# A streamed weight's low half made by an adding transfer instead of a subtraction, and two output-projection tiles interleaved

## The chip, the cores and the metric

The kernel runs on one core of a Trainium2 chip. The metric is the device time of one execution in microseconds; before the change it is 893.74 us, the median of 3 runs (893.54 to 894.2).

## The reference

One layer of a streaming encoder on 512 positions with 1024 channels. Two branches share a normalised input and one input projection: an RWKV-7 recurrence and a chunked gated delta rule. Their outputs are projected, gated, summed and sent through an output projection; then follow a gated MLP with a causal convolution and a last norm. Cut to what matters here, the matrix products:

```
u = rms_norm(x, norm1_g);  p = u @ w_in                       # 1024 x 5888 and a few columns
y_a = rwkv7_mix(p_rwkv, ...) @ rwkv_proj                       # 512 x 1024
y_b = gated_deltanet_mix(qkv, z, ...) @ gdn_proj               # 512 x 1024
mixed = sigmoid(gate_a) * y_a + sigmoid(gate_b) * y_b
x = x + mixed @ w_out                                          # 1024 x 1024
h = causal_depthwise_conv(rms_norm(x, norm2_g) @ ffn_up, w)    # 1024 x 5632
x = x + (silu(h_gate) * h_up) @ ffn_down                       # 2816 x 1024
return rms_norm(x, final_g)
```

All of it is float32. Each large product is computed in three passes of a shorter float format (float32r): a number a is split into a high half, a rounded to that format, and a low half, a minus the high half. The kernel adds low x high, high x high and high x low.

## The kernel before

Everything is kept transposed: channels on the 128 partitions, the 512 positions along the free dimension. A large product goes tile by tile: 128 output channels at a time, whose weights for all inputs are one tile of 128 x 1024 floats (512 KB), called a unit.

`unit` (lines 162 to 170) streams one unit. SP loads it into `raw`, a ring of two buffers. Then for each 512 columns `halves_of` (lines 152 to 160) makes the two halves: ScalarE copies to `hi` (line 156), and the subtraction raw - hi gives `lo` (line 158), every second one on GpSimd and the others on VectorE. `hi` and `lo` are rings of four buffers (HB = 4), that is two units' worth. `mm3` (line 173 on) then runs 12 matmuls for each such half: for each of the four input blocks low x high (line 180) and high x high (line 181), then four times high x low (line 183). So the first matmul of a half needs its `lo`.

The order of the program is: the first tiles (`first_tiles`), a hand-written order of recurrence steps, gates and projections in `mixing` (the table ORDER), the two branch projections (`project`), the output projection (`merge`, lines 967 on), 44 tiles of up-projection (`causal_conv3`), and the down projection (`down_pair`), which takes four pairs of output tiles; a part of it is a fast matrix product with `pair_weights`, the rest (`plain`) streams units whose last half has only 256 columns. The very last output tile is computed in two halves of 256 positions, so that its result can be normalised and stored in two pieces. A scheduler sets each engine's order; most of `unit` runs at high priority, ahead of its place in the program, as far as the rings allow. Each engine works through its own queue in order, and an instruction that waits holds up those behind it.

In `merge` the eight output tiles come one after the other, each with both of its halves. Their input `uh`, `ul` is the sum of the gated branches, made channel block by channel block by the second branch projection: the first half of a tile needs blocks 0 to 3, the second 4 to 7.

Of the kernel before, what the change touches and what calls it, by code (L numbers as in the profile page):

```python
# [9 lines left out]
F32 = mybir.dt.float32  # L10
F32R = mybir.dt.float32r
BF16 = mybir.dt.bfloat16
AF = mybir.ActivationFunctionType
ALU = mybir.AluOpType
# [3 lines left out]
D = 1024  # L18
# [76 lines left out]
class Body:  # L95
# [53 lines left out]
        self.second = False  # L149


    def halves_of(self, raw, o, w=512):
        nc = self.nc
        hi = self.stream.tile([128, 512], F32R, tag="hi", name=self.nm("hi"), bufs=HB)
        lo = self.stream.tile([128, 512], F32R, tag="lo", name=self.nm("lo"), bufs=HB)
        nc.scalar.activation(hi[:, 0:w], raw[:, o:o + w], AF.Copy)  # L156
        self.halves += 1
        self.on(str(self.halves % 4)).tensor_tensor(out=lo[:, 0:w], in0=raw[:, o:o + w], in1=hi[:, 0:w].bitcast(F32),  # L158
                                                    op=ALU.subtract)
        return hi, lo, w // 128  # L160

    def unit(self, src, n=1024, ahead=True):
        nc = self.nc
        parts = []
        with self.tc.high_priority() if ahead else nullcontext():
            raw = self.stream.tile([128, 1024], F32, tag="raw", name=self.nm("raw"), bufs=2)
            nc.sync.dma_start(out=raw[:, 0:n], in_=src)
            for o in range(0, n, 512):
                parts.append(self.halves_of(raw, o, min(512, n - o)))
        return parts  # L170


# [779 lines left out]
    def merge(self):  # L952
        nc, tc = self.nc, self.tc
        x1 = self.x1 = self.x1p.tile([128, KD, T], F32, name="x1")
        self.acc2 = self.x1p.tile([128, T], F32, name="acc2")
        for k in range(KD):
            nc.sync.dma_start(out=x1[:, k, :], in_=self.a["xT"][k])
        mh, ml = self.uh, self.ul
        with tc.tile_pool(name="proj", bufs=1, reuse_waits="tile") as pp:
            yh = pp.tile([128, 4, T], F32R, name="yh")  # L960
            yl = pp.tile([128, 4, T], F32R, name="yl")
            for i in range(4):
                self.split(yh[:, i, :], yl[:, i, :], self.yf[:, 4 + i, :], scale=0.5)
            self.project(1, lambda k: (yh[:, k, :], yl[:, k, :]))
        self.u2p = self.pool("u2p", bufs=1, reuse_waits="tile")
        self.u2h = self.u2p.tile([128, KD, T], F32R, name="u2h")
        self.u2l = self.u2p.tile([128, KD, T], F32R, name="u2l")
        for m in range(KD):
            parts = self.unit(self.a["w_out"][m])
            ps = self.bank("D")  # L970
            self.mm3(ps, parts, lambda k: (mh[:, k, :], ml[:, k, :]))
            x = x1[:, m, :]
            g = self.vec("norm2", m)
            with tc.high_priority():
                nc.vector.tensor_tensor(out=x, in0=ps, in1=x, op=ALU.add)
                nc.scalar.activation(self.u2h[:, m, :], x, AF.Copy, scale=g)
                nc.vector.scalar_tensor_tensor(out=self.u2l[:, m, :], in0=x, scalar=g, in1=self.u2h[:, m, :].bitcast(F32),
                                               op0=ALU.mult, op1=ALU.subtract)
            self.sumsq(self.acc2, x, m == 0)
# [267 lines left out]
```

## Time and profile before

| what | value |
|---|---|
| median of 3 runs | 893.74 us |
| the profiled execution | 897.17 us |
| its span, first to last instruction | 895.0 us |
| TensorE busy | 860.9 us, 96% |
| VectorE busy | 646.0 us, 72% |
| ScalarE busy | 473.2 us, 53% |
| GpSimd busy | 209.7 us, 23% |
| transfers, mean over the span | 94 GB/s |

The profile comes from one execution. Busy times say how much of the span an engine had an instruction running; matmuls overlap, so a busy TensorE may still have room. Where an engine's idle time is named with another engine, that one's instruction came last. PE is TensorE, DVE is VectorE, ACT is ScalarE, POOL is GpSimd, SP issues the transfers.

### The profile page before, as it was taken

How to read it: one execution, taken by the hardware profiler on the slowest of the kernel's cores; microseconds unless marked ns; L12 is line 12 of the kernel's file. 1: busy time of each engine (PE TensorE's matmuls, PEld its weight loads, DVE VectorE, ACT ScalarE, POOL GpSimd, SP SyncE). 2: the span in 40 equal slices, each digit the busy share in tenths (PEclk: the TensorE clock that was granted, in tenths of full speed). 3: DMA queues.
4: the chain of work that ended last, by engine and by line, in shares of the span. 5: the costliest groups of instructions: out<-in, count | busy, mean ns of one | idle time of the engine just before them, and what ended most of it. 6: DMA issues, size and time to landing. Idle time of an engine off the chain costs nothing.

```text
span 895.0 us, 13509 instructions
## 1 busy us (share of the span) xinstructions
PE 860.9 (96%) x5046; PEld 677.9 (76%) x5046; DVE 646.0 (72%) x1247; ACT 473.2 (53%) x909; POOL 209.7 (23%) x189
## 2 busy tenths in 40 slices
PE   7989999999999999999999999999999999999996
PEld 4867677666767777667787878888888888898895
DVE  6898797874888986855476448988866666573565
ACT  7745457667443777673543455455444444444433
POOL 2231123111121221111212222222222222352431
PEclk9999999999999999999999999999999999999998
DMA  7321222121212221125352323323333332332333
GB/s 263 112 91 59 71 71 72 48 73 48 72 59 71 71 72 37 60 89 206 94 174 85 94 95 94 95 94 95 94 100 101 101 100 90 99 102 86 110 86 133
DMA packets 29746, 84.25 MB, mean 94 GB/s; under 512 B 3312, under 2 KB 5488, under 8 KB 29680
## 3 DMA queue, kind: packets, MB, share of 16 engines
q1 hardware_dynamic: 29680, 83.39, 29.3%
q8 instruction: 40, 0.66, 0.3%
q14 instruction: 26, 0.21, 0.1%
HBM read 77.61 MB, written 5.77 MB: 93 GB/s over the span
## 4 chain that ended last, share of the span: by engine, by line
PE 70%; DVE 19%; ACT 4%; issue 4%; DMA 1%; POOL 1%; SPq 0%; DVEq 0%; POOLq 0%; ACTq 0%
PE D L183 15%; PE D L180 15%; PE D L181 15%; PE D L1077 5%; PE A L1077 4%; PE B L1077 3%; DVE lo L158 2%; DVE R L534 1%; DVE P L769 1%; DMA raw<-w_in 1%; DVE invN L563 1%; DVE BK L513 1%; DVE invY L565 1%; DVE BK L508 1%; DVE R L948 1%
## 5 line engine op out<-in xcount | busy, mean ns | idle before, releaser
L158 POOL TENSOR_TENSOR lo<-raw,hi 128x512 fp32r<-128x512 f32 x124 | 170.3, 1373 | 614.4 <-ACT hi L156 590.6
L156 ACT ACTIVATE hi<-raw 128x512 fp32r<-128x512 f32 x248 | 152.9, 620 | 195.7 <-PE D L183 95.2
L180 PE MATMUL D<-uh,lo 128*128 128x512 f32 x384 | 158.3, 413 | 3.5 <-ACT uh L204 1.9
L181 PE MATMUL D<-uh,hi 128*128 128x512 f32 x384 | 157.6, 410 | 0.0
L180 PE MATMUL D<-u2h,lo 128*128 128x512 f32 x352 | 137.9, 392 | 0.0
L181 PE MATMUL D<-u2h,hi 128*128 128x512 f32 x352 | 137.8, 392 | 0.0
L183 PE MATMUL D<-ul,hi 128*128 128x512 f32 x384 | 117.8, 411 | 0.4 <-DVE ul L202 0.4
L158 DVE TENSOR_TENSOR lo<-raw,hi 128x512 fp32r<-128x512 f32 x124 | 87.7, 707 | 34.9 <-ACT hi L156 34.5
L183 PE MATMUL D<-u2l,hi 128*128 128x512 f32 x352 | 95.1, 392 | 0.0
L180 PEld LDWEIGHTS D<-uh,lo 128*128 128x128 f32 x384 | 72.7, 189 | 21.8 <-ACT uh L204 2.4
L181 PEld LDWEIGHTS D<-uh,hi 128*128 128x128 f32 x384 | 72.6, 189 | 16.0 <-issue 1.0
L994 DVE SCALAR_TENSOR_TENSOR P<-T,vecs,P 128x511 f32<-128x511 f32 x88 | 78.3, 890 | 8.4 <-ACT P L992 4.1
L183 PEld LDWEIGHTS D<-ul,hi 128*128 128x128 f32 x384 | 70.4, 189 | 17.1 <-issue 1.2
L181 PEld LDWEIGHTS D<-u2h,hi 128*128 128x128 f32 x352 | 66.1, 188 | 14.9 <-issue 0.2
L180 PEld LDWEIGHTS D<-u2h,lo 128*128 128x128 f32 x352 | 66.1, 188 | 14.7 <-issue 0.2
L183 PEld LDWEIGHTS D<-u2l,hi 128*128 128x128 f32 x352 | 66.1, 188 | 14.1
L991 DVE TENSOR_TENSOR T<-D,acc 128x512 f32<-128x512 f32 x44 | 30.3, 688 | 34.5 <-PE D L183 30.6
L992 ACT ACTIVATE P<-T,vecs 128x512 f32<-128x512 f32 x44 | 31.7, 721 | 12.1 <-DVE T L991 10.0
L563 DVE TENSOR_TENSOR invN<-invA,invY 128x60 f32<-128x60 f32 (+24 forms) x124 | 33.2, 268 | 2.6
L565 DVE TENSOR_TENSOR invY<-invY,invN 128x60 f32<-128x60 f32 (+24 forms) x124 | 33.0, 266 | 2.9
L769 DVE SCALAR_TENSOR_TENSOR P<-D,vecs,P 128x511 f32<-128x511 f32 (+2 forms) x36 | 26.6, 740 | 1.5 <-ACT P L767 1.5
L1183 ACT ACTIVATE P<-P 128x512 f32<-128x512 f32 x22 | 13.7, 624 | 18.7 <-DVE P L994 18.7
(437 smaller groups left out, 1566.1 us busy)
## 6 DMA issues: line engine op xcount, KB each, us to landing
raw<-w_in SPq DMA_DIRECT2D x44, 512.0 KB, 3.5
raw<-ffn_up SPq DMA_DIRECT2D x44, 512.0 KB, 3.6
raw<-ffn_down SPq DMA_DIRECT2D x9, 512.0 KB, 3.5
raw<-w_out SPq DMA_DIRECT2D x8, 512.0 KB, 3.6
raw<-ffn_down SPq DMA_DIRECT2D x16, 256.0 KB, 2.9
spill<-T SPq DMA_DIRECT2D x14, 256.0 KB, 2.0
R<-spill SPq DMA_DIRECT2D x14, 256.0 KB, 5.9
raw<-ffn_down SPq DMA_DIRECT2D x9, 384.0 KB, 3.1
```

The costliest lines, as they stand in the source:

```text
L156: nc.scalar.activation(hi[:, 0:w], raw[:, o:o + w], AF.Copy)
L158: self.on(str(self.halves % 4)).tensor_tensor(out=lo[:, 0:w], in0=raw[:, o:o + w], in1=hi[:, 0:w].bitcast(F32), op=ALU.subtract)
L180: nc.tensor.matmul(ps, wl[:, w[k]], x[k][0], start=(first and i == 0 and k == 0), stop=False)
L181: nc.tensor.matmul(ps, wh[:, w[k]], x[k][0], start=False, stop=False)
L183: nc.tensor.matmul(ps, wh[:, w[k]], x[k][1], start=False, stop=(last and i == len(parts) - 1 and k == n - 1))
L563: nc.vector.tensor_tensor(out=w, in0=rows[:, t, 0:t].unsqueeze(2).broadcast_to([128, t, n]), in1=Ym[:, t, c:G].unsqueeze(1).broadcast_to([ ...
L565: nc.vector.tensor_tensor(out=Ym[:, 0:t, c:G], in0=Ym[:, 0:t, c:G], in1=w, op=ALU.add)
L769: nc.vector.scalar_tensor_tensor(out=cv[:, sh:], in0=ps[:, 0:T - sh], scalar=w(3 - sh), in1=cv[:, sh:], op0=ALU.mult, op1=ALU.add)
L991: nc.vector.tensor_tensor(out=h, in0=ps, in1=self.acc2, op=ALU.mult)
L992: nc.scalar.activation(cv, h, AF.Copy, scale=w(2))
L994: nc.vector.scalar_tensor_tensor(out=cv[:, sh:], in0=h[:, 0:T - sh], scalar=w(2 - sh), in1=cv[:, sh:], op0=ALU.mult, op1=ALU.add)
L1077: nc.tensor.matmul(out, w, x, start=bank not in started, stop=stop)
```

## The change

Two edits. In `halves_of` a `lo` that belongs to a streamed unit is no longer a subtraction. ScalarE writes minus `hi` into the `lo` buffer, and GpSimd's queue issues a transfer that reads the same weights once more from HBM and adds them to what stands in that buffer. `unit` passes the source for this. The first two tiles of the kernel, which call `halves_of` themselves, keep the subtraction (four halves). All others, 244 halves, go the new way; GpSimd and VectorE lose their part in them.

In `merge` the first two output tiles are interleaved: the first half of tile 0, the first half of tile 1, then the second halves.

```
-    def halves_of(self, raw, o, w=512):
+    def halves_of(self, raw, o, w=512, src=None):
         ...
         nc.scalar.activation(hi[:, 0:w], raw[:, o:o + w], AF.Copy)
+        if src is not None:
+            nc.scalar.activation(lo[:, 0:w], hi[:, 0:w].bitcast(F32), AF.Copy, scale=-1.0)
+            nc.gpsimd.dma_start(out=lo[:, 0:w], in_=src[:, o:o + w], accum_op=ALU.add)
+            return hi, lo, w // 128
         self.halves += 1
         self.on(str(self.halves % 4)).tensor_tensor(out=lo[:, 0:w], in0=raw[:, o:o + w], in1=hi[:, 0:w].bitcast(F32),
                                                     op=ALU.subtract)
...
-                parts.append(self.halves_of(raw, o, min(512, n - o)))
+                parts.append(self.halves_of(raw, o, min(512, n - o), src))
...
+        mixed = lambda k: (mh[:, k, :], ml[:, k, :])
+        two = [(self.unit(self.a["w_out"][m]), self.bank("D")) for m in range(2)]
+        for q in range(2):
+            for parts, ps in two:
+                self.mm3(ps, parts[q:q + 1], lambda k: mixed(4 * q + k), first=q == 0, last=q == 1)
         for m in range(KD):
-            parts = self.unit(self.a["w_out"][m])
-            ps = self.bank("D")
-            self.mm3(ps, parts, lambda k: (mh[:, k, :], ml[:, k, :]))
+            if m < 2:
+                ps = two[m][1]
+            else:
+                parts = self.unit(self.a["w_out"][m])
+                ps = self.bank("D")
+                self.mm3(ps, parts, mixed)
```

Where it moves instructions, first on ScalarE near the start of the program, before. Here `hi_240` and `hi_244` are the two halves of the first streamed unit, `hi_319` and `hi_323` those of the second, `hi_366` the first of the third; P is the input's norm, T and `sg` are the first two shifted projections, `xw` and `xa` what is made of T.

```order
L156 ACTIVATE hi_240<-raw_238 128x512
L156 ACTIVATE hi_244<-raw_238 128x512
L312 ACTIVATE lora_h<-w2a_236 128x1024
L195 ACT_TABLE_LOAD
L195 ACTIVATE P_101<-A_265,cons 128x512
L196 ACT_TABLE_LOAD
L196 ACTIVATE P_101<-P_101 128x512
L156 ACTIVATE hi_319<-raw_317 128x512
L156 ACTIVATE hi_323<-raw_317 128x512
L372 ACTIVATE T_269<-T_270,omu 128x512
L156 ACTIVATE hi_366<-raw_364 128x512
L372 ACTIVATE sg<-T_279,omu 128x512
```

The same place on ScalarE now, from the second streamed unit on, whose halves are called 321 and 326, with their `lo` 322 and 327:

```order
L157 ACTIVATE hi_321<-raw_319 128x512
L157 ACTIVATE hi_326<-raw_319 128x512
L377 ACTIVATE T_271<-T_272,omu 128x512
L159 ACTIVATE lo_322<-hi_321 128x512
L377 ACTIVATE sg<-T_281,omu 128x512
L326 ACTIVATE T_271<-T_271 64x512
L328 ACTIVATE xa<-T_271 64x512
L328 ACTIVATE xw<-T_271 64x512
L331 ACTIVATE sg<-sg 128x512
L159 ACTIVATE lo_327<-hi_326 128x512
L377 ACTIVATE P_288<-T_315,omu 128x512
```

The minus copies (L159) have come into ScalarE's queue; the first unit's two stand directly behind its `hi`, the second unit's `lo_322` behind one copy and `lo_327` behind five more instructions.

In the up-projection, on ScalarE, two tiles before (P is the convolution's sum and its silu, `ah` the high half of the gated product):

```order
L156 ACTIVATE hi_5967<-raw_5965 128x512
L201 ACTIVATE ah<-P_5829 128x512
L156 ACTIVATE hi_5971<-raw_5965 128x512
L992 ACTIVATE P_5915<-T_5914,vecs 128x512
L156 ACTIVATE hi_6008<-raw_6006 128x512
L1183 ACTIVATE P_5915<-P_5915 128x512
L156 ACTIVATE hi_6012<-raw_6006 128x512
```

And two tiles now:

```order
L157 ACTIVATE hi_6127<-raw_6125 128x512
L159 ACTIVATE lo_6128<-hi_6127 128x512
L206 ACTIVATE ah<-P_5983 128x512
L157 ACTIVATE hi_6132<-raw_6125 128x512
L159 ACTIVATE lo_6133<-hi_6132 128x512
L1007 ACTIVATE P_6073<-T_6072,vecs 128x512
L157 ACTIVATE hi_6170<-raw_6168 128x512
L159 ACTIVATE lo_6171<-hi_6170 128x512
L1198 ACTIVATE P_6073<-P_6073 128x512
L157 ACTIVATE hi_6175<-raw_6168 128x512
L159 ACTIVATE lo_6176<-hi_6175 128x512
```

Each `lo` stands directly behind the `hi` of its half, and everything else keeps its place. On GpSimd 244 transfers stand where 122 subtractions stood, in the order of the halves.

On TensorE, the start of the output projection before: `D_4720` and `D_4759` are the sums of tiles 0 and 1, `hi_4712` and `hi_4716` the halves of tile 0's weights (the rows between are the other matmuls of the same half):

```order
L183 MATMUL B_4687<-yl,hi_4666 128x512 x4
L180 MATMUL D_4720<-uh,lo_4713 128x512
...
L183 MATMUL D_4720<-ul,hi_4712 128x512 x4
L180 MATMUL D_4720<-uh,lo_4717 128x512
...
L183 MATMUL D_4720<-ul,hi_4716 128x512 x4
L180 MATMUL D_4759<-uh,lo_4752 128x512
```

And now, where tile 0 is `D_4826` and tile 1 `D_4839`:

```order
L188 MATMUL B_4791<-yl,hi_4769 128x512 x4
L185 MATMUL D_4826<-uh,lo_4817 128x512
...
L188 MATMUL D_4826<-ul,hi_4816 128x512 x4
L185 MATMUL D_4839<-uh,lo_4830 128x512
...
L188 MATMUL D_4839<-ul,hi_4829 128x512 x4
L185 MATMUL D_4826<-uh,lo_4822 128x512
```

The first half of tile 1 has moved ahead of the second half of tile 0.

## Rows read from the trace of the kernel before

**Rows 1.** The page: busy time by engine, and the chain that ended last by engine.

```profile
PE 860.9 (96%) x5046; PEld 677.9 (76%) x5046; DVE 646.0 (72%) x1247; ACT 473.2 (53%) x909; POOL 209.7 (23%) x189
PE 70%; DVE 19%; ACT 4%; issue 4%; DMA 1%; POOL 1%; SPq 0%; DVEq 0%; POOLq 0%; ACTq 0%
```

**Rows 2.** Busy time by stretch: us, busy of each engine, clock, DMA share, GB/s.

```profile
50.00:400.00 350.00, 332.29 (x2519) 244.09 (x2520) 281.47 (x717) 211.50 (x475) 62.92 (x75) 1.00 0.20 64
...
400.00:456.00 56.00, 56.00 (x293) 43.72 (x292) 26.85 (x50) 28.71 (x51) 9.97 (x8) 1.00 0.46 156
456.00:482.00 26.00, 24.06 (x106) 19.37 (x104) 21.89 (x30) 9.43 (x17) 5.71 (x4) 1.00 0.43 142
482.00:712.00 230.00, 230.00 (x993) 187.59 (x994) 163.75 (x224) 112.11 (x182) 58.54 (x42) 0.99 0.32 96
```

**Rows 3.** The page's groups: count, busy us, mean ns, idle before.

```profile
L158 POOL TENSOR_TENSOR lo<-raw,hi 128x512 fp32r<-128x512 f32 x124 | 170.3, 1373 | 614.4 <-ACT hi L156 590.6
L156 ACT ACTIVATE hi<-raw 128x512 fp32r<-128x512 f32 x248 | 152.9, 620 | 195.7 <-PE D L183 95.2
...
L158 DVE TENSOR_TENSOR lo<-raw,hi 128x512 fp32r<-128x512 f32 x124 | 87.7, 707 | 34.9 <-ACT hi L156 34.5
```

**Rows 4.** TensorE's waits, 50 to 400 us: us in total, times, longest.

```profile
PE A L517 <- DVE P L515: 5.2, 4, 2.0
...
PE B L907 <- DVE vn L905: 0.2, 1, 0.2
```

**Rows 5.** The page's DMA issues: count, KB each, median us to landing.

```profile
raw<-ffn_up SPq DMA_DIRECT2D x44, 512.0 KB, 3.6
...
raw<-ffn_down SPq DMA_DIRECT2D x16, 256.0 KB, 2.9
...
R<-spill SPq DMA_DIRECT2D x14, 256.0 KB, 5.9
```

**Rows 6.** Timeline of TensorE, first and second streamed unit: start, us, instruction.

```profile
22.12 0.80 PE L180 MATMUL A<-gh,lo 128*128 128x512 f32 x1
...
28.03 0.39 PE L180 MATMUL A<-gh,lo 128*128 128x512 f32 x1
```

**Rows 7.** Timeline of ScalarE over the same stretch.

```profile
17.36 1.14 ACT L156 ACTIVATE hi<-raw 128x512 fp32r<-128x512 f32 x2
...
25.26 1.14 ACT L156 ACTIVATE hi<-raw 128x512 fp32r<-128x512 f32 x2
...
29.55 0.64 ACT L321 ACTIVATE T<-T 64x512 f32<-64x512 f32 x1 [1.40 <-DVE T L373]
```

**Rows 8.** Timeline in the up-projection: TensorE at two halves' starts, ScalarE between.

```profile
651.43 0.39 PE L180 MATMUL D<-u2h,lo 128*128 128x512 f32 x1
...
654.18 0.39 PE L180 MATMUL D<-u2h,lo 128*128 128x512 f32 x1
...
651.63 0.63 ACT L156 ACTIVATE hi<-raw 128x512 fp32r<-128x512 f32 x1 [0.81 <-PE D L183]
```

**Rows 9.** Timeline of VectorE, one line twice; GpSimd subtracts from 469.91.

```profile
467.96 0.68 DVE L948 TENSOR_TENSOR R<-R,R 128x512 f32<-128x512 f32 x1
...
469.96 1.80 DVE L948 TENSOR_TENSOR R<-R,R 128x512 f32<-128x512 f32 x1
...
469.91 1.30 POOL L158 TENSOR_TENSOR lo<-raw,hi 128x512 fp32r<-128x512 f32 x1 [5.00 <-ACT hi L156]
```

**Rows 10.** Timeline of TensorE in the last two output tiles.

```profile
872.53 0.62 PE L1077 MATMUL A<-ah,lo 128*128 128x512 f32 x2
...
873.90 0.63 PE L1077 MATMUL B<-ah,lo 128*128 128x256 f32 x4
...
876.73 0.63 PE L1077 MATMUL B<-ah,lo 128*128 128x256 f32 x4
878.14 0.40 PE L1077 MATMUL B<-ah,lo 128*128 128x256 f32 x2
...
882.75 0.63 PE L1077 MATMUL D<-ah,lo 128*128 128x256 f32 x4
```

**Rows 11.** Groups by line: GpSimd's subtraction in the fast matrix product.

```profile
L1046 POOL TENSOR_TENSOR u2l<-P,u2h 128x512 fp32r<-128x512 f32 x8 | 12.2, 1530 | 13.7 <-ACT u2h L1045 13.7
```

## The prediction

> **What bounds the kernel now.** I read the page first. TensorE is busy 96% of the span and ends 70% of the chain of waits; VectorE, busy 72%, ends 19% [rows 1]. Next the busy time by stretch [rows 2]: from 400 to 456 us and from 482 to 712 us TensorE's busy time equals the stretch, so freeing VectorE or GpSimd there is worth nothing. Before that it is idle: 350.00 - 332.29 = 17.7 us between 50 and 400 us, and 26.00 - 24.06 = 1.94 us at 456 to 482 us, where VectorE is busy 281.47 of 350 us and 21.89 of 26 us. TensorE's waits between 50 and 400 us name VectorE in ten rows, from 5.2 us down to 0.2 us, 11.0 us together [rows 4]. That is what a lighter VectorE can give back; the rest of the 17.7 us hangs on ScalarE or on no wait that the profile shows.
>
> The second thing to see is the ring of four buffers. A half of a weight tile (12 matmuls of 512 columns) takes 654.18 - 651.43 = 2.75 us on TensorE, and ScalarE starts the next `hi` at 651.63, 0.20 us after the following half began, that is as soon as the buffer is free [rows 8]. A half's `hi` and `lo` must be ready when three further halves are done: 3 x 2.75 = 8.25 us after the buffer was freed. Whatever making a `lo` takes within that is hidden.
>
> **The change part by part.** It removes 122 of 124 VectorE subtractions, 122 x 0.707 = 86 us, and 122 of 124 on GpSimd, 122 x 1.373 = 168 us; it adds 244 ScalarE passes at about 0.62 us, 151 us on an engine that was busy 473 us [rows 1, 3], and 244 transfers from GpSimd's queue. ScalarE then stands near 70%, so its total isn't the bound, but its order is.
>
> *The new path of a `lo`.* From the freed buffer: 0.20 us to the start of `hi`, two passes of 0.63 us one behind the other, and about 0.08 us for the hand-over, 1.54 us together [rows 8]; then T, from GpSimd's issue to the landing. No row shows T: GpSimd issues no transfer in this trace, and none accumulates. Lower bound: a 256 KB load issued by SP lands after 2.9 us. Upper bound: the 256 KB reloads that stand in a crowd land after 5.9 us [rows 5]. A transfer that adds must read 256 KB in HBM and 256 KB in SBUF, so the nearest row is the 512 KB load with 3.6 us; GpSimd's handling comes on top, between nothing and one of its passes of 1.37 us [rows 3, 5]. I take 3.6 + 0.8 = 4.4 us, which is also the middle of the two ends. So L = 1.54 + 4.4 = 5.9 us, against 8.25 us of cover.
>
> The Trainium skill speaks against a cheap T: "Collectives: The Full Stack", section "The bandwidth ceiling: the fold count and why AG ≠ RS ≠ AR", says that a reducing transfer runs at half the rate of a copy because it reads two sources. No run here shows it yet; with it the data part of T is that of the 512 KB row, without it that of the 256 KB row, 0.7 us less, and the sum below would fall by about 2 x 0.7 us at the tail and 0.7 us at the start.
>
> *Start of the kernel, +6.0 us.* Here nothing runs ahead. The first streamed unit's two `hi` end at 18.50 us, its first `lo` pass at 19.1, and the transfer lands at 23.5; TensorE wanted it at 22.12 [rows 6, 7]: 1.4 us late. The second unit's two `hi` start at 25.26; by the new order one copy and then its first `lo` follow, done at 27.6, landed at 32.0, wanted at 28.03 + 1.4 = 29.4: 2.6 us. Its second `lo` stands behind a tanh that started at 29.55 because it waits for VectorE, and behind three more passes, so it is done at about 32.4 and lands at 36.8, wanted at 32.0 + 2.75: 2.0 us. Later units have their `lo` passes early enough. VectorE's work on the shifted projections waits for these products, so I count all 6.0 us.
>
> *50 to 400 us, -7.0 us.* VectorE loses its subtractions, and it also loses a collision: the same addition on two SBUF operands takes 0.68 us alone and 1.80 us while GpSimd subtracts [rows 9]. Against this stands ScalarE, which gets a further pass for every half. Bounds: 0 and the 11.0 us of [rows 4]; I take two thirds, since the largest wait in it, 5.2 us, is of the kind that VectorE's load sets.
>
> *Output projection, -1.9 us.* The first tile waited 1.94 us for the last merged channels [rows 2]; with two first halves ahead, 5.5 us of other matmuls stand before that need. Nothing is late in its place: both tiles' four halves fill the ring, which they did before.
>
> *Projections at 400 to 456 us, +2.0 us.* The reloads of the spilled gates share the transfer engines (share 0.46 [rows 2]) and themselves land after 5.9 us. The stretch holds five turns of the ring. Bounds: 0 if T stays 4.4 us, 5 us if each turn is late by 1 us; I take 2.
>
> *Up-projection, 0.* 44 tiles, all with 8.25 us of cover. ScalarE's queue holds `hi` and then `lo` of the same half with nothing between. If L passes 8.25 us this cover is gone: 22 turns, each late by the excess.
>
> *Down projection, +1.0 us.* Its last half has 6 matmuls, 873.90 - 872.53 = 1.37 us [rows 10], so the cover is 2.75 + 2.75 + 1.37 = 6.87 us, 0.9 us more than L. Four turns follow one another without a long block between. GpSimd's queue also holds subtractions of 1.5 us [rows 11]; where one stands ahead of a transfer that half is 0.6 us late, in two turns of four.
>
> *Last tile, +3.1 us.* It runs in two column halves, and a weight half lasts only 878.14 - 876.73 = 1.41 us. The buffer freed at 872.53 is wanted again at 876.73, and its successor at 882.75 [rows 10]. The first can start at 872.53 + L, the next at 872.53 + L + 1.41 + L; that is 2L - 8.81 us after 882.75, 3.1 us for L = 5.94. Nothing follows that could hide it.
>
> **Sum.** 6.0 - 7.0 - 1.9 + 2.0 + 0 + 1.0 + 3.1 = +3.2 us. The profiled execution took 897.17 us with a span of 895.0 us, 0.4% above the median of 893.74 us; I add the difference to the median: 896.9 us.
>
> **The rivals.**
>
> *The transfer is as quick as a plain load (faster).* Place: start and tail. With T = 2.9 us L is 4.4: the start costs 0 + 2.5 + 2.0 = 4.5 us, the tail 0.1 us, projections and down projection nothing, and VectorE's whole 11.0 us come back: 4.5 - 11.0 - 1.9 + 0.1 = -8.3 us, 885.4 us. For it: SP's 256 KB row, and transfer engines that are idle two thirds of the time [rows 2, 5]. Against it: the transfer isn't SP's, and it adds. It decides when T is under about 4.0 us. The Trainium skill is on its side: "DMA: Bandwidth & Descriptors", section "Anatomy of one DMA — SWDGE (gpsimd) path", gives 2.0 us plus bytes over 436 GB/s for a transfer issued from GpSimd, an estimate of 2.6 us here; no run here shows it so far.
>
> *The ring of four is too short (clearly slower).* With T = 5.9 us L is 7.4: start 2.9 + 2.6 + 2.0 = 7.5, only -4.0 between 50 and 400 us, -1.9, projections +5.0, down projection 4 x 0.57 + 1.0 = 3.3, tail 6.1: +16.0 us, 909.7 us. From T = 6.7 us the up-projection joins: at T = 7.0 us start 8.6, -2.0, -1.9, +8.0, 22 x 0.3 = 6.5, down projection 7.7, tail 8.3: +35.2 us, 928.9 us. For it: the reloads' 5.9 us, each `lo` now shares the transfer engines with the next tile's 512 KB, and each weight is read from HBM twice. Against it: between 482 and 712 us the engines' share is only 0.32 [rows 2].
>
> *The interleaving does nothing.* If the last merged channels come more than 5.5 us after the first half could start, the wait stays: 1.9 us more, 898.8 us. In the row it was 1.94 us, so I hold this for unlikely and inside the forecast's range.
>
> **How the numbers follow.** Forecast (T between 4.0 and 5.0 us, 891 to 902 us): 40%. Quick transfer: 33%. Too short a ring: 27%. What a measurement tells from no change here is about 0.2%, 1.8 us; of the forecast's 40% some 13 lie within that, 27 above. So faster 33%, same 13%, slower 54%. The range goes from the quick case to the far end of the slow one, 885 to 928 us.
>
> **What would show it.** TensorE: waits on `lo` in the first 45 us of some 6 us and in the last 15 us of some 3 us, none between 530 and 700 us. VectorE between 50 and 400 us: busy 250 us or less instead of 281, and no addition at 1.8 us. The issue table: a line for `lo` with about 3.5 to 4.5 us to landing. The forecast is wrong if that line shows under 3 us or over 5.5 us, if the first wait for `lo` is missing, or if TensorE's idle time between 50 and 400 us stays at 17 us.

## The result and the profile after

Four runs of the changed kernel took 921.84 to 924.57 us, median 923.33, beside 893.97 us for the kernel before: ratio 1.0323, interval 1.0299 to 1.0346, slower. The profiled execution has a span of 922.7 us against 895.0, 27.7 us more, where the sum of the prediction had +3.2. The time lies in the range, but at the place of the rival "the ring of four is too short" (909.7 to 928.9 us), not of the forecast (891 to 902 us).

Where the 27.7 us went is read from the matmuls that read a `lo`. Of before (each row: line, engine, operands, count, shortest/median/longest in ns, first and last start in us):

```profile
L180 PE MATMUL D<-uh,lo x384: 388/396/798, 45.0 to 522.8; 128*128 128x512 f32 x192
L180 PE MATMUL D<-u2h,lo x352: 387/392/792, 524.2 to 765.4; 128*128 128x512 f32 x176
L1077 PE MATMUL D<-ah,lo x70: 278/388/467, 766.8 to 884.3; 128*128 128x512 f32 x56, 128*128 128x256 f32 x14
L180 PE MATMUL B<-yh,lo x32: 388/392/397, 453.7 to 474.3; 128*128 128x512 f32 x32
...
L180 PE MATMUL A<-invN,lo x16: 391/392/398, 431.4 to 451.4; 128*128 128x512 f32 x16
```

and the same rows of after:

```profile
L185 PE MATMUL D<-uh,lo x384: 387/395/802, 55.2 to 530.1; 128*128 128x512 f32 x192
L185 PE MATMUL D<-u2h,lo x352: 388/392/792, 531.5 to 774.5; 128*128 128x512 f32 x176
L1092 PE MATMUL D<-ah,lo x70: 276/392/796, 775.8 to 912.1; 128*128 128x512 f32 x56, 128*128 128x256 f32 x14
L185 PE MATMUL B<-yh,lo x32: 388/392/474, 460.4 to 484.3; 128*128 128x512 f32 x32
...
L185 PE MATMUL A<-invN,lo x16: 392/397/766, 431.5 to 458.1; 128*128 128x512 f32 x16
```

These starts cut the span into stages: start to the first `D<-uh`, mixing to the first `A<-invN`, projections to the last `B<-yh`, output projection to the first `D<-u2h`, up-projection to the first `D<-ah`, and the rest. Differences of the starts give:

| stage | before | after | change | forecast |
|---|---|---|---|---|
| start | 45.0 | 55.2 | +10.2 | +6.0 |
| mixing | 386.4 | 376.3 | -10.1 | -7.0 |
| projections | 42.9 | 52.8 | +9.9 | +2.0 |
| output projection | 49.9 | 47.2 | -2.7 | -1.9 |
| up-projection | 242.6 | 244.3 | +1.7 | 0 |
| down projection and last tile | 128.2 | 146.9 | +18.7 | +4.1 |

The gains came, somewhat larger than forecast. The losses are 40.5 us instead of 12.1, most of them in the projections and the down projection. The page after, its busy line and the queue of the new transfers:

```profile
PE 874.8 (95%) x5046; PEld 685.6 (74%) x5046; DVE 519.1 (56%) x1125; ACT 612.1 (66%) x1153; POOL 253.5 (27%) x311
...
q0 software_dynamic: 35136, 62.80, 41.9%
```

The same 5046 matmuls are busy 874.8 us instead of 860.9 [rows 1]: half of the net loss, 13.9 us, is not waiting but slower matmuls. The other half, 13.8 us, is idle time. TensorE's waits name whom it waited for:

```profile
PE D L1092 <- DMA lo<-ffn_down: 6.1, 4, 3.2
PE A L185 <- DMA lo<-w_in: 6.1, 2, 3.3
PE B L1092 <- DMA lo<-ffn_down: 5.8, 4, 2.9
PE A L185 <- DMA lo<-rproj: 3.6, 1, 3.6
...
PE B L185 <- DMA lo<-gproj: 2.5, 3, 1.4
...
PE D L185 <- DMA lo<-ffn_up: 1.2, 1, 1.2
```

(us in total, times, longest.) VectorE's rows of before, 11.0 us between 50 and 400 us [rows 4], have shrunk to 5.6 us; transfers of `lo` stand in their place, at start, projections and down. Behind the longest of them the clock is low. Stretches of after (width, then busy time of PE, PEld, DVE, ACT and POOL, then granted clock, share of the transfer engines, GB/s):

```profile
24.00:30.00 6.00, 5.71 (x14) 4.51 (x15) 3.42 (x5) 5.50 (x10) 0.96 (x2) 0.51 0.66 148
41.00:46.00 5.00, 5.00 (x12) 3.95 (x13) 1.05 (x2) 0.11 (x1) 0.89 (x1) 0.50 0.94 217
...
445.00:450.00 5.00, 5.00 (x14) 3.85 (x14) 0.69 (x1) 0.79 (x2) 0.00 (x0) 0.53 0.64 116
...
50.00:400.00 350.00, 340.04 (x2572) 251.30 (x2570) 249.68 (x692) 260.46 (x566) 81.08 (x116) 1.00 0.57 126
```

The first three lie behind waits of 3.3, 2.8 and 3.6 us: from the end of the wait on TensorE is busy all the time, at 0.50 to 0.53, the lower of its two levels (1.2 of 2.4 GHz), with 12 to 14 matmuls in 5 to 6 us. The last one answers to [rows 2]: TensorE idle 10.0 us instead of 17.7, VectorE 249.7 us instead of 281.5. The transfers, KB each and median us from issue to landing:

```profile
lo<-w_in POOLq DMA_DIRECT2D x88, 256.0 KB, 4.6
raw<-ffn_up SPq DMA_DIRECT2D x44, 512.0 KB, 5.1
lo<-ffn_up POOLq DMA_DIRECT2D x88, 256.0 KB, 4.8
lo<-ffn_down POOLq DMA_DIRECT2D x27, 256.0 KB, 5.2
...
lo<-gproj POOLq DMA_DIRECT2D x8, 256.0 KB, 5.7
```

and over all 244 of them:

```profile
DMA to landing us min/median/max: 3.5/4.8/8.9
```

The forecast had T = 4.4 us. A T of 4.8 everywhere would have moved my sum by some 2 us, so more than 20 us have another source. One is the spread of T. Another is shown by the third half of a tile of the down projection (start, length, engine and line, [idle before, and what ended it]). ScalarE:

```profile
846.50 0.63 ACT L157 ACTIVATE hi<-raw 128x512 fp32r<-128x512 f32 x1 [1.45 <-PE D L1092]
847.16 0.63 ACT L159 ACTIVATE lo<-hi 128x512 fp32r<-128x512 f32 x1
849.24 0.63 ACT L157 ACTIVATE hi<-raw 128x512 fp32r<-128x512 f32 x1 [1.45 <-PE D L1092]
851.86 0.63 ACT L1060 ACTIVATE u2h<-raw 128x512 fp32r<-128x512 f32 x1 [1.99 <-DMA raw<-ffn_down]
852.40 0.62 ACT L159 ACTIVATE lo<-hi 128x512 fp32r<-128x512 f32 x1
```

GpSimd:

```profile
848.20 0.89 POOL L160 DMA_DIRECT2D lo<-ffn_down  x1 [1.89 <-ACT lo L159]
852.58 1.48 POOL L1061 TENSOR_TENSOR u2l<-raw,u2h 128x512 fp32r<-128x512 f32 x1 [3.49 <-ACT u2h L1060]
854.00 1.77 POOL L160 DMA_DIRECT2D lo<-ffn_down  x2
```

TensorE:

```profile
853.66 1.20 PE L1092 MATMUL D<-ah,lo 128*128 128x512 f32 x4 [0.33 <-DMA lo<-ffn_down]
859.85 2.08 PE L1092 MATMUL D<-ah,lo 128*128 128x512 f32 x4 [3.15 <-DMA lo<-ffn_down]
```

In the second half nothing stands between the steps, and its `lo` is still used only 7.2 us after its `hi` (846.50 to 853.66): the issue starts 0.4 us behind the copy's end where I had 0.08, and the transfer lands about 5.4 us after that. The third half has its `hi` at 849.24, but ScalarE's next instruction is a `u2h` of the following block, which waits for a load until 851.86; the minus copy stands behind it (852.40). GpSimd then works on that block's subtraction first (852.58) and issues at 854.00. The half is usable at 859.85, 10.6 us after its `hi` began, and the matmuls behind it are slow (2.08 us for four, 1.07 at full clock).

Most waits have no such blocked copy. The longest of the projections:

```profile
436.04 0.62 ACT L157 ACTIVATE hi<-raw 128x512 fp32r<-128x512 f32 x1
436.69 0.63 ACT L159 ACTIVATE lo<-hi 128x512 fp32r<-128x512 f32 x1
437.73 0.87 POOL L160 DMA_DIRECT2D lo<-rproj  x1 [6.68 <-ACT lo L159]
443.68 0.77 PE L185 MATMUL A<-invN,lo 128*128 128x512 f32 x1 [3.65 <-DMA lo<-rproj]
```

The steps follow one another at once, and T is 5.8 us. But ScalarE, at work without a break since 424.0 us, among others on four table loads of 1.28 us, comes to this `hi` only at 436.04, 4.0 us before TensorE wants the half (443.68 - 3.65 = 440.03), not 8.25. The same timelines of the down projection show a blocked copy behind two of its eight waits (2.2 and 3.2 us of 11.9); behind the other six, 6.5 us, the copy starts 0.66 us after its `hi`, the issue 0.4 us after the copy, and T is 4.3 to 7.0 us.

### The profile page after: what moved, and what is told of

It is laid out like the page before. It is cut to its first block, busy times and chain, and to the rows that moved or that the text cites. A ratio compares the mean times of both kernels' runs of the same rounds, so it can differ in the third digit from the quotient of the medians.

```text
span 922.7 us, 13967 instructions
## 1 busy us (share of the span) xinstructions
PE 874.8 (95%) x5046; PEld 685.6 (74%) x5046; DVE 519.1 (56%) x1125; ACT 612.1 (66%) x1153; POOL 253.5 (27%) x311
## 3 DMA queue, kind: packets, MB, share of 16 engines
q0 software_dynamic: 35136, 62.80, 41.9%
## 4 chain that ended last, share of the span: by engine, by line
PE 66%; issue 10%; DMA 9%; ACT 7%; DVE 6%; POOL 2%; SPq 0%; POOLq 0%; DVEq 0%; ACTq 0%
PE D L188 16%; PE D L185 16%; PE D L186 15%; PE D L1092 4%; DMA lo<-ffn_down 3%; PE B L1092 2%; PE A L1092 2%; POOL lo L160 2%; DMA lo<-w_in 1%; DVE R L539 1%; DMA lo<-gproj 1%; ACT hi L157 1%; DMA raw<-ffn_down 1%; ACT lo L159 1%; PE B L666 1%
## 5 line engine op out<-in xcount | busy, mean ns | idle before, releaser
L160 POOL DMA_DIRECT2D lo<-w_in x88 | 77.3, 887 | 298.0 <-ACT lo L159 139.2
L186 PE MATMUL D<-uh,hi 128*128 128x512 f32 x384 | 157.4, 410 | 0.0
L159 ACT ACTIVATE lo<-hi 128x512 fp32r<-128x512 f32 x244 | 151.0, 621 | 5.6
L186 PE MATMUL D<-u2h,hi 128*128 128x512 f32 x352 | 137.5, 391 | 0.0
L160 POOL DMA_DIRECT2D lo<-ffn_up x88 | 76.5, 870 | 168.1 <-PE D L185 145.4
L188 PE MATMUL D<-ul,hi 128*128 128x512 f32 x384 | 115.1, 408 | 0.0
L1009 DVE SCALAR_TENSOR_TENSOR P<-T,vecs,P 128x511 f32<-128x511 f32 x88 | 66.0, 750 | 50.1 <-ACT P L1007 48.4
L186 PEld LDWEIGHTS D<-uh,hi 128*128 128x128 f32 x384 | 72.6, 189 | 16.7 <-issue 1.4
L186 PEld LDWEIGHTS D<-u2h,hi 128*128 128x128 f32 x352 | 66.1, 188 | 14.7 <-issue 0.2
L160 POOL DMA_DIRECT2D lo<-ffn_down x36 | 31.5, 891 | 58.2 <-ACT lo L159 31.5
L570 DVE TENSOR_TENSOR invY<-invY,invN 128x60 f32<-128x60 f32 (+24 forms) x124 | 28.8, 232 | 2.9
L568 DVE TENSOR_TENSOR invN<-invA,invY 128x60 f32<-128x60 f32 (+24 forms) x124 | 28.4, 229 | 2.9
```

What stands on the lines that cost most here:

```text
L159: nc.scalar.activation(lo[:, 0:w], hi[:, 0:w].bitcast(F32), AF.Copy, scale=-1.0)
L160: nc.gpsimd.dma_start(out=lo[:, 0:w], in_=src[:, o:o + w], accum_op=ALU.add)
L186: nc.tensor.matmul(ps, wh[:, w[k]], x[k][0], start=False, stop=False)
L188: nc.tensor.matmul(ps, wh[:, w[k]], x[k][1], start=False, stop=(last and i == len(parts) - 1 and k == n - 1))
L568: nc.vector.tensor_tensor(out=w, in0=rows[:, t, 0:t].unsqueeze(2).broadcast_to([128, t, n]), in1=Ym[:, t, c:G].unsqueeze(1).broadcast_to([ ...
L570: nc.vector.tensor_tensor(out=Ym[:, 0:t, c:G], in0=Ym[:, 0:t, c:G], in1=w, op=ALU.add)
```

## The experiments

All ran beside the kernel before on the same chip; ratios are to it. The runs were made in four groups, in which the kernel before has medians of 893.6 to 894.7 us, so a difference between runs of two groups is good to about 1 us. "Stage" numbers are differences of the starts in the table above against the profile of before.

**The interleaving alone** (the source is not handed on, so every half subtracts):

```
-                parts.append(self.halves_of(raw, o, min(512, n - o), src))
+                parts.append(self.halves_of(raw, o, min(512, n - o)))
```

> The kernel before with the second edit alone: the first two tiles of the output projection interleaved, all subtractions as before. Theory (the two edits are independent): the output projection lost 1.94 us to a wait before and loses none now, and the changed kernel took 2.7 us less than before between the start of the output projection and the first matmul of the up-projection; so -1.9 to -2.7 us, some 891 to 892 us, and no row for a wait of D on uh at 475 us. Rival (the gain there came from a VectorE without subtractions): the wait stays in part and the time is that of before within 1 us, 893 to 895 us.

891.53 us, ratio 0.996 [0.9947, 0.9973]. The wait of the first tile (it ends at 482 us) is gone and the output projection gives 3.7 us: the 1.94 us of idle time, and the low clock behind it; TensorE is busy 53.00 of 53.00 us at a clock of 1.00 from 466 to 519 us, where it had 0.97 before (475 to 524 us). The theory held, and even here the wait had cost twice. The adding transfers alone therefore lose about 32 us.

**Subtraction in the down projection** of the changed kernel:

```
+                self.adding = False
                 parts = self.unit(self.a["ffn_down"][m1 + j][:, k0 * 128:(k0 + w) * 128], w * 128)
```

> The changed kernel, but the plain tiles of the down projection (36 halves) make their lo by subtraction as before. Theory (the down projection's loss is its own: its transfers stand behind blocked instructions on ScalarE and GpSimd, and its short halves leave little cover): the 18.7 us that the stretch from the first down-projection matmul to the end is longer than before come back, 923.3 - 18.7 = 904.6 us, give or take 1.5. Rival (the transfer engines, whose share went from about 0.3 to 0.89, slow everything near them, also what the earlier stages left behind): less than half comes back, 914 us or more.

903.48 us, ratio 1.0095 [1.0076, 1.0113]; down projection +0.1 us instead of +18.7, the earlier stages as in the changed kernel (projections +10.5). Its loss was its own.

**Adding transfers in the mixing stage alone**, interleaved (a flag that the first projection tile takes back):

```
                 first = self.first_tiles(xp)
+            self.adding = True
...
+            self.adding = False
             parts = self.unit(self.a["gproj" if j else "rproj"][m2])
```

> Adding transfers only for the units of the mixing stage (between 45 and 430 us); the start, the projections, the output, up- and down projection subtract as before; the output projection interleaved. Theory (each stage's gain and loss is its own): start and down as before, the mixing stage keeps its 10.1 us and the output projection its 2.7 us: 894.0 - 12.8 = 881 us, 880 to 884. Rival (the mixing stage only caught up what the start had lost, since its end is set by VectorE's chain and not by where it began): with no late start there is nothing to catch up, and the time is 888 to 893 us.

884.8 us, ratio 0.9887 [0.9872, 0.9902], a little above the theory's 880 to 884 us. Mixing -9.4 us, output -3.8, all later stages 0: the gain wasn't a catching-up. Three waits on `lo`, 5.3 us together, remain; whether they are what is missing from 12.8 us is asked further down.

**A copy in place of the adding**:

```
-            nc.gpsimd.dma_start(out=lo[:, 0:w], in_=src[:, o:o + w], accum_op=ALU.add)
+            nc.gpsimd.dma_start(out=lo[:, 0:w], in_=src[:, o:o + w])
```

> The changed kernel with a transfer from GpSimd that copies the weights over minus the high half instead of adding to it: lo then holds the whole weight, so the sum of the parts is left out. Same 256 KB, same queue, same order, no adding. Theory (the adding, which reads two sources, is what is dear): the landing falls from 4.8 us to 3.6 us or less, lo's share of the transfer engines from 41.9% to about 21%, and the time by some 10 us, 910 to 916 us. Rival (the way from GpSimd's issue through its descriptors is what is dear): the landing stays at 4.4 to 4.8 us and the time at 920 to 924 us.

Here `lo` holds the whole weight: this kernel leaves out the sum of the parts. 893.48 us, ratio 0.9996 [0.9985, 1.0008]: 29.9 us below the changed kernel, three times what the theory said; down projection +4.4 us, start +3.6, projections +3.5. The rows that answer to those of after:

```profile
q0 software_dynamic: 35136, 62.80, 25.7%
...
lo<-w_in POOLq DMA_DIRECT2D x88, 256.0 KB, 3.3
...
lo<-ffn_up POOLq DMA_DIRECT2D x88, 256.0 KB, 3.2
lo<-ffn_down POOLq DMA_DIRECT2D x27, 256.0 KB, 3.7
```

Adding costs 1.3 to 1.6 us a transfer, and for the same 62.80 MB 0.419 x 922.7 = 387 us of the engines' time instead of 0.257 x 890.9 = 229. That these 1.5 us make 30 us of the whole fits a kernel that stands just beyond the edge of its cover. The run changes two things at once, T and the load of the engines, and doesn't tell them apart.

**Zeros in the wait** of the changed kernel:

```
+        for i in range(fill):      # 14 ahead of tile 4, 12 ahead of tile 8
+            self.nc.tensor.matmul(ps, self.zero[:, 0:128], self.zero, start=(i == 0), stop=False)
```

> The changed kernel with 14 matmuls of zeros (128x512, bf16) ahead of the first streamed tile and 12 ahead of the third, into the same accumulation, where TensorE waits 3.3 and 2.8 us for a lo; nothing else. Theory (a wait for a lo costs twice, since TensorE is granted half its clock for some 5 us behind it: 0.51 from 24 to 30 us, 0.50 from 41 to 46 us): with the zeros it stays near 1.00, each of the two tiles gives back some 2.5 us, and the first matmul of the mixing stage starts at about 50 us instead of 55.2; the time falls by what the mixing stage does not swallow, 918 to 922 us. Rival (the low clock there has another cause, or the lo that follow are late anyway): the start of the mixing stage stays within 1 us of 55.2, and the time at 922 to 924 us.

918.31 us, ratio 1.0274 [1.0247, 1.03], 4 to 5 us under the changed kernel. The two stretches with the same limits:

```profile
24.00:30.00 6.00, 5.26 (x23) 3.87 (x22) 4.07 (x6) 5.94 (x12) 0.87 (x1) 1.00 0.73 155
...
41.00:46.00 5.00, 5.00 (x24) 4.09 (x23) 1.60 (x3) 1.93 (x4) 0.97 (x2) 1.00 0.70 164
```

The clock is 1.00 in both, 24 matmuls stand where 12 stood, and the mixing stage begins at 52.1 us instead of 55.2: the low clock follows from the idle time. Of the forecast 5 us in that stretch 3.1 came. The down projection, which the edit doesn't touch, was 3.8 us shorter in this execution, so not all of the difference is to be put down to the zeros.

**The minus copy first, and from the loaded tile**:

```
-        nc.scalar.activation(hi[:, 0:w], raw[:, o:o + w], AF.Copy)
         if src is not None:
-            nc.scalar.activation(lo[:, 0:w], hi[:, 0:w].bitcast(F32), AF.Copy, scale=-1.0)
+            nc.scalar.activation(lo[:, 0:w], raw[:, o:o + w], AF.Copy, scale=-1.0)
             nc.gpsimd.dma_start(out=lo[:, 0:w], in_=src[:, o:o + w], accum_op=ALU.add)
+            nc.scalar.activation(hi[:, 0:w], raw[:, o:o + w], AF.Copy)
```

> The changed kernel with the minus copy made straight from the loaded tile and ahead of the high half (one pass of 0.63 us sooner, and no instruction can stand between the two for want of the other). Theory (in the down projection a lo is late because its minus copy stands behind a u2h that waits for a load, hi at 784.3 and 849.2 us but lo usable only at 793.8 and 859.9): these two waits of 2.2 and 3.2 us go, with the low clock behind them, and every other wait loses 0.65 us; the down projection falls from +18.7 to about +8 us against before, the start and the projections by 1 to 2 us each, the whole to 908 to 912 us. Rival (the landing of 4.8 to 5.7 us is what is late, wherever the copy stands): the two waits stay above 1.5 us, only 0.65 us a wait comes back, 916 to 920 us.

900.37 us (896.84 to 903.44), ratio 1.0071 [1.0038, 1.0103]: 23 us back, more than the theory's 11 to 15, with T nearly the same (4.3, 4.5 and 4.8 us for `w_in`, `ffn_up` and `ffn_down`). Start +6.2 us, mixing -7.9, projections +1.4, up-projection +0.1, down +8.0. What the theory had missed can be read on ScalarE in the up-projection:

```profile
556.80 0.63 ACT L158 ACTIVATE lo<-raw 128x512 fp32r<-128x512 f32 x1 [0.22 <-PE D L186]
557.87 0.63 ACT L160 ACTIVATE hi<-raw 128x512 fp32r<-128x512 f32 x1 [0.44 <-PE D L189]
559.48 0.63 ACT L158 ACTIVATE lo<-raw 128x512 fp32r<-128x512 f32 x1 [0.97 <-PE D L186]
560.62 0.63 ACT L160 ACTIVATE hi<-raw 128x512 fp32r<-128x512 f32 x1 [0.51 <-PE D L189]
```

The `lo` starts when the last matmul that reads the old `lo` (L186) is done, the `hi` 1.1 us later, when the last four that read the old `hi` (L189) are. A minus copy that reads `hi` waits for both; taken from the tile it comes 1.1 + 0.67 = 1.8 us sooner. One blocked half is left in the down projection (2.1 us): the short half's copy still stands behind a `u2h`.

**The up-projection alone**:

```
+        self.adding = True
         parts = self.unit(self.a["ffn_up"][j])
+        self.adding = False
```

> Adding transfers for the up-projection's tiles alone, subtraction everywhere else, the output projection interleaved. Theory (a cover of three halves, 8.25 us, hides it): the time is that of the interleaving alone, 891.5 us, plus at most 2 us for the first tile, though the transfer engines' share there goes from 0.32 to about 0.9; 891 to 894 us, no row of waits on lo longer than 1.5 us. Rival (engines at 0.9 of their time are a bound of their own, hidden so far behind the earlier stages' delay): 896 us or more, with waits on lo spread over the 44 tiles.

893.79 us, ratio 0.9994 [0.9979, 1.0009], up-projection +1.5 us with one wait of 1.2 us on `lo`, the engines' share at 0.7 to 0.9 through the stage. (The execution is 3.0 us longer than that of the interleaving alone; the other 1.5 us lie in the mixing stage, which this edit doesn't touch.) 88 adding transfers on nearly full engines are hidden by 8.25 us of cover; a bound of the engines is ruled out here.

**Mixing alone, the minus copy first**, and the stage's first tile subtracted:

```
+        add = self.adding and self.skip == 0
+        self.skip -= self.adding and self.skip > 0
```

> The version with adding transfers in the mixing stage alone (884.8 us), with the minus copy made straight from the loaded tile and ahead of the high half, and the first tile of the stage still subtracted. Theory (its three waits on lo, 5.3 us together, are one of the first tile, whose lo lands 6.8 us after issue, and one of a minus copy that stands behind a G that waits 2.4 us, at 115 to 119 us): both go, 880 to 882 us. Rival (the stage's end is set by VectorE's chain, which these waits do not lengthen): 884 to 886 us.

884.37 us, ratio 0.9892 [0.987, 0.9914]. The three waits on `lo` went, the time did not: the rival held. Something other than `lo` ends that stage.

**Mixing stage: all subtractions on GpSimd, or all on VectorE**, no adding transfers, interleaved (`"1"` GpSimd, `"0"` VectorE):

```
-        self.on(str(self.halves % 4)).tensor_tensor(
+        self.on(self.only or str(self.halves % 4)).tensor_tensor(
```

> The kernel before with the interleaving, and in the mixing stage every subtraction for a lo on GpSimd instead of every second one; no adding transfers. VectorE loses the same work as with the adding transfers, but GpSimd's 1.37 us passes on SBUF operands double. Theory (the mixing stage's gain of 8 to 10 us is VectorE's freed time): as with the adding transfers, 882 to 885 us. Rival (the gain is the end of the collisions, an addition of 1.80 us instead of 0.68 while GpSimd subtracts): no gain against the interleaving alone, 891 us or more, and more slow VectorE instructions.

915.35 us, ratio 1.0239 [1.0209, 1.027], mixing +23.9 us: the theory is wrong, and the rival, which allowed anything from 891 us up, was too mild. TensorE's longest waits are on VectorE (3.9, 2.7 and 2.5 us), none on a `lo` from GpSimd: VectorE's freed time is worth nothing beside GpSimd's passes.

> The same with every subtraction of the mixing stage on VectorE: it gets 40 passes of 0.7 us more, and GpSimd's passes and their collisions are gone. Theory (VectorE's load sets the waits): some 40 x 0.7 = 28 us more on an engine that is busy 80% of the stage, 895 to 905 us. Rival (the collisions are what costs): 883 to 888 us, VectorE's busy time in the stage not above the 281 us of before.

884.75 us, ratio 0.9895 [0.9879, 0.9912]; mixing and projections together -7.2 us (the projections' first matmuls come among the last of the mixing here, so the two are taken as one), as with the transfers (-8.0 in the run before these two). My theory was wrong and the rival right. Subtractions on VectorE between 50 and 400 us and the stage's busy time, with the interleaving alone:

```profile
L163 DVE TENSOR_TENSOR lo<-raw,hi 128x512 fp32r<-128x512 f32 x36 | 24.6, 684 | 1.4 <-ACT hi L157 1.4
...
L518 DVE TENSOR_TENSOR BK<-P,T 64x256 f32<-64x256 f32 x16 | 8.7, 543 | 0.2
```

```profile
50.00:400.00 350.00, 334.16 (x2539) 245.20 (x2539) 280.21 (x717) 212.72 (x480) 63.57 (x75) 1.00 0.21 66
```

and with all on VectorE:

```profile
L164 DVE TENSOR_TENSOR lo<-raw,hi 128x512 fp32r<-128x512 f32 x75 | 51.4, 685 | 14.5 <-ACT hi L158 13.7
...
L520 DVE TENSOR_TENSOR BK<-P,T 64x256 f32<-64x256 f32 x16 | 6.7, 418 | 0.2
```

```profile
50.00:400.00 350.00, 340.30 (x2555) 250.69 (x2554) 281.63 (x754) 210.53 (x482) 13.05 (x35) 1.00 0.22 68
```

VectorE takes 39 more passes, 26.8 us, and is busy 281.6 us instead of 280.2: its other work shrank by 25.4 us (the multiplication x16 goes from 543 to 418 ns), with GpSimd at work for 13 us beside it instead of 64. That GpSimd's subtractions are the cause, other rows say as well: the neighbouring product from three operands (`BK<-P,sp,T`, 64x256) takes 480 ns here, 538 with the interleaving alone and 717 with all subtractions on GpSimd (the multiplication itself stays at 545 there); and with the adding transfers, where GpSimd is busy 79 us with issuing, the multiplication takes 419 ns.

**All subtractions on VectorE in every stage**, and **the same with adding transfers in the mixing stage** (minus copy first, the stage's first tile subtracted), both interleaved:

```
-        self.on(str(self.halves % 4)).tensor_tensor(
+        nc.vector.tensor_tensor(
```

> The kernel before with the interleaving and every streamed tile's subtraction on VectorE, in all stages; no adding transfers, none on GpSimd. Theory (outside the mixing stage VectorE is not waited for): the time of the version with VectorE alone in the mixing stage, 884.8 us, within 1.5 us, since projections, up- and down projection keep TensorE busy either way. Rival (the projections, where VectorE was busy 29.6 of 44 us, or the down projection become VectorE-bound): 887 us or more, with waits on lo at 420 to 466 us or behind 766 us.

882.34 us, ratio 0.9857 [0.9833, 0.988], 1 us below the theory's range.

> The best version so far with adding transfers in the mixing stage (884.4 us) and every remaining subtraction on VectorE, so that no subtraction for a lo runs on GpSimd at all. Theory (what the transfers gain is the end of the collisions, and VectorE alone gives the same): nothing to add, 883 to 885.5 us, equal to the version without transfers. Rival (freed time and ended collisions add up): 881 us or less.

881.95 us, ratio 0.9854 [0.9834, 0.9874], 1 us below the theory's range and 1 us above the rival's. The two are equal: the gains don't add up. Either both remove the same thing, as the 418 and 419 ns suggest, or both end at the same next limit; the runs don't tell these apart. The first of the two beats the kernel before by 1.4% with no adding transfer and nothing read twice.

## Why the prediction was right in sign and wrong in size

**The new path of a `lo`: the step that failed.** "L = 1.54 + T = 5.9 us, against 8.25 us of cover." L was 7.2 us in an undisturbed half of the down projection and 10.6 in a blocked one, and the cover was 4.0 us at the longest wait of the projections. Four things were mis-sized. T was taken as one number: its medians are 4.6 to 5.7 us, but single transfers took 3.5 to 8.9 us; 17 of the 52 of both projections and the down projection passed my upper bound of 5.9 us, and 3 of the 88 of the up-projection. The issue starts 0.4 us after the copy and not 0.08. I had seen that GpSimd's subtractions can stand ahead and priced that at 0.6 us, but not that a waiting instruction of the next block can stand between `hi` and minus copy. And a full ring is no cover where ScalarE begins late. The run with the minus copy first starts each path sooner and brought 23 of 29 us back at nearly the same T; the copy in place of the adding shortens T by 1.3 to 1.6 us and brought 30 us back with the queues as they were. Either takes most of the loss, since the cover is missed by little; neither takes all (8.0 and 4.4 us remain in the down projection).

**The range held by luck.** The forecast itself (891 to 902 us, 40%) failed; its sum of +3.2 us is about a ninth of the 27.7 of the profiled executions. The time lies in the range because that reaches to the far end of the short ring. The signs of being wrong that the prediction names don't catch it: the 4.6 to 5.2 us of the large groups of `lo` lie inside the 3 to 5.5 us that it allowed, since it asked for a median and not for the spread.

**A wait was priced at its length.** Idle time was half of the net loss; slower matmuls cost as much again, behind three of the longest waits at clocks of 0.50 to 0.53. This term is in none of my stages; the zeros showed it in the first, where 3.1 us came back. It applies to the gain too (output projection: 1.9 forecast, 3.7 us by itself).

**Start, +6.0; it was +10.2.** That the waits are those forecast in sum (6.1 us) is luck: they are 3.3 us at the first tile, where I had 1.4, and 2.8 at the third, where I had none; the second, with 4.6 forecast, had none. The rest goes with the low clock behind them.

**50 to 400 us, -7.0; the stage gave -10.1.** The size was near (between 50 and 400 us TensorE's idle time fell by 7.7 us), and of my two reasons the one I named second is the right one: not VectorE's lost subtractions but the collision [rows 9]. Full GpSimd and full VectorE subtraction tell them apart by 31 us. VectorE's 249.7 us were forecast (250 or less), and the additions of 1.8 us are gone, as forecast: the line of [rows 9] takes 691 ns each of its eight times.

**Projections, +2.0; it was +9.9.** One half came 3.6 us late with a low clock behind it (0.53 from 445 to 450 us), above all because ScalarE began it late, and three by 2.5 us together, two of them with a T of 7.2 and 7.4 us. My bound of 5 us had neither a late `hi` nor the clock in it.

**Up-projection, 0; it was +1.7.** Nearly right: 8.25 us hide all but one of 88 halves, with a wait of 1.2 us (T was 6.0 us) where I had forecast none, and by itself the stage costs 1.5 us.

**Down projection and tail, +1.0 and +3.1; together +18.7.** The largest error: eight waits of 11.9 us together, and 6.8 us more of busy time for the same matmuls. The last tile has 4.7 us of these waits, at a T of 4.3 to 7.0 us, where I had 3.1; 5.4 us stand behind two blocked copies, the rest is 1.8 us. Place and part of the cause (short halves, subtractions in GpSimd's queue) were named, the size wasn't.

**The rivals.** The short ring had the right mechanism, a path longer than its cover, and came nearer than my forecast at the start, in the projections and in the down projection. Its condition, T of 5.9 us or more, was met by a third of the transfers of the last two and hardly elsewhere; what else lengthened L it didn't have, and it gave the mixing stage 4.0 or 2.0 us of gain where that gained 10.1. The quick transfer is answered by the copy: at T of 3.2 to 3.7 us it still took 893.48 us, 8 us above that rival's 885.4, with 4.4 us left in the down projection, so even T near its lower bound would not have paid. The Trainium skill ("Collectives: The Full Stack", section "The bandwidth ceiling: the fold count and why AG ≠ RS ≠ AR") states for collectives that a reducing one runs at about half the rate of a copying one because the add reads two sources. This transfer isn't a collective; the runs agree in direction: engine time 387 against 229 us, a factor of 1.7 where half rate would be 2. Its price for a transfer from GpSimd ("DMA: Bandwidth & Descriptors", section "Anatomy of one DMA — SWDGE (gpsimd) path"), an estimate of 2.6 us here, lies under the 3.2 us of the copy and the 4.6 of the adding.

What stays open: how the 18.7 us of the down projection divide between blocked queues, long transfers and the clock (executions differ there by some 4 us), what makes single transfers take 7 to 9 us, and what ends the mixing stage now.

## What to carry to other kernels

Price a new producer from the freed buffer to the landing as the queues run it, with every instruction that can stand ahead of it and between its steps and with the spread of a transfer's time, not its median, and not as a sum of latencies; where the cover is missed by a microsecond or two, add to the wait the low clock behind it. Break needless links first: a copy that reads the source instead of another copy's result, and so can go first, was worth 23 us. And before work is moved off a busy engine, ask whether it is the load or a neighbour that makes it busy: here giving VectorE more work and GpSimd less gained as much as taking the work away.

## What the runs showed that was not expected

Adding against copying, both from GpSimd at 256 KB: medians of 4.6 to 5.2 us against 3.2 to 3.7 us to the landing in the three large groups, and 1.7 times the engines' time for the same bytes; single adding transfers took 3.5 to 8.9 us. The issue itself holds GpSimd for 0.86 to 0.89 us. Three idle stretches of 2.8 to 3.6 us on TensorE were followed by some 5 us at half the clock each, and zeros in two of these waits prevented it there. A VectorE multiplication of 64x256 took 543 ns on average beside GpSimd's subtractions, 418 ns without them, and 419 ns while GpSimd issued transfers instead.
